# Hybrid decoder layer on one Trainium2 core: wider shift products and a tied order in the first stage, and five smaller moves behind it

## The chip, the core and the metric

The kernel runs on one core of a Trainium2 chip. The engines that matter are TensorE (PE; its weight loads are listed apart as PEld), VectorE (DVE), ScalarE (ACT), GpSimd (POOL, used here for fills and for issuing DMAs) and SyncE (SP, which issues most DMAs). They run side by side and wait for one another through semaphores. The metric is the device time of one execution in microseconds (us); lower is better. One profiled execution gives a trace with every instruction on every engine.

## The reference

One layer (DEPTH = 1) over 1024 tokens of width 1024: a mixing sub-layer that runs a convolution module and stick-breaking attention on one modulated input, then a SwiGLU sub-layer; all is float32.

```python
c_act = jax.nn.silu(c)
mod = c_act @ ada_w[l] + ada_b[l]
sh1, sc1, ga1, sh2, sc2, ga2 = [m[:, None, :] for m in jnp.split(mod, 6, axis=-1)]
h = rmsnorm(x, pre_mix_g[l]) * (1.0 + sc1) + sh1
y = hybrid_mixer(h, ...)
x = x + ga1 * rmsnorm(y, post_mix_g[l])
h = rmsnorm(x, pre_ffn_g[l]) * (1.0 + sc2) + sh2
y = swiglu_ffn(h, w_ffn_in[l], w_ffn_out[l])
x = x + ga2 * rmsnorm(y, post_ffn_g[l])
...
def hybrid_mixer(h, ...):
    proj = h @ w_in
    glu_in, qkv, gates = jnp.split(proj, [2 * CONV_WIDTH, 2 * CONV_WIDTH + 3 * ATT_WIDTH], axis=-1)
    ...
    merged = jax.nn.sigmoid(g_conv) * y_conv + jax.nn.sigmoid(g_att) * y_att
    return merged @ w_o
```

## The kernel before

Activations are kept transposed: 8 tiles of 128 channels by 1024 tokens, and a product works on one stationary block of 128 x 128 weights and 512 tokens (a chunk c, of two). For precision each float32 operand is split into a rounded part (hi, type float32r, made on ACT) and the remainder (lo, made on DVE), and a product is the sum of three: hi x hi, hi x lo and lo x hi. In the text these are named HH (weight hi, activation hi), HL (weight hi, activation lo) and LH (weight lo, activation hi). Plain float32 products (sums with a block of ones, shift products, convolution) go through PE in two records each.

The stages, in order of time:

- **First stage**, up to about 67 us. ACT squares the tiles of x, PE sums them over the channels with a block of ones (pvar). For each of the 8 channel tiles k a 1 MB tile of the conditioning weights (ada_w, `aws[k]`, five buffers) gives a shift and a scale. The scales of all k, and the shifts of k = 5 to 7 (SH_DVE), are dot products on DVE (`dots`, line 121). The shifts of k = 0 to 4 are made on PE: `shift_pe(k)` (L280) runs eight products of 128 x 128 weights with one moving column, and `shift_act(k)` (L284) adds the bias. `x_op` (DVE, L296) scales x, `hi_op` (ACT, L299) and `lo_op` (DVE, L302) make the split operand of h, and `gemm_k` (L317) multiplies it with three weight tiles: the first of Q, of K and of the gate of the convolution's GLU (q0b, k0b, gg0b; the weights are `w0s`). The loop over k does Q, K and gate of one k, each in the order HH, HL, LH. `pin` chains the instructions of an engine in the order of the program text, so that the planner can't reorder them; in this stage only DVE and ACT are pinned.
- **Attention and convolution**, to about 415 us. `qk_pair` copies Q and K out of PSUM (L499 to L516), `v_half` (L478) makes V with two weight tiles that `load_w` splits (L145, L155), `head` does the attention, `glu` and `conv` the convolution module.
- **Gates**, from about 410 us on. Two of the sixteen gate tiles are made plainly (PLAIN, L622) and stored to DRAM (`s_d`, L101); the other seven pairs go through a scheme with seven instead of eight block products (`early`, L635, and `other_five`, L704 to L731), in which the planner mixes the layer norm of the convolution (`ln_all`).
- **Projections**: `y_conv` (L747) with four weight tiles `wc`, the attention's projection, then w_o (L919). A weight tile goes through three rotations of three buffers each: raw ("wraw"), hi ("whi") and lo ("wlo"). The gate operands of `other_five` use the same "whi" and "wlo" buffers.
- **FFN**, from about 740 us. Its beginning is written out by hand and pinned on PE, DVE and ACT. While the second half of the tokens is still being normalised, PE makes early products for 11 of the 22 blocks: `ke(f, i)` (L1109) multiplies one weight tile with four operand tiles, and `e(f, i)` (L1114) copies the result out and stores it. The sums T1 to T4 of the seven-product scheme are made by `t12`, `t3` (L1134), `t4` with `hi_of` (ACT, L1119) and `lo_of` (DVE, L1123). `ffn(f)` is a generator: each `next(r0)` does one more step of block 0 (operands s2o, then s1o and s3o, then the products, L1001).
- **Last stage**, from about 1170 us: the second FFN product in four sweeps; the first, "pa", uses `prep1`, which splits two weight parts (`wop2`, L1535) and two activation parts (`op2`, L1529; L145 for both hi parts).

Outside the pinned pieces a planner orders every engine's instructions from a simulated timeline, with priorities that follow the program text. Each engine then runs its instructions strictly in that order. DMAs are issued by SP (loads, `load`), POOL (stores, `store`, L101) or ACT (`act.dma_start`).

## Time and profile before

| | |
|---|---|
| median of 3 runs | 1400.02 us (1399.16 to 1400.69) |
| the profiled execution | 1400.8 us |
| span in the profile (first to last instruction) | 1399.0 us |
| mean granted clock of PE over the span | 0.994 |
| instructions | 18714 |
| read from and written to HBM | 192.74 MB and 71.04 MB |

The times of the profile are counted from the span's start. A line of a timeline gives start, duration, engine, source line, operation, written and read tiles, shapes and count; in brackets stands the idle time of the engine before it and what ended it. PE's matmuls overlap, so the start of one to the start of the next is its cost, not its duration.

### The profile page before, as it was taken

What the parts mean: (1) busy time and instruction counts of PE and PEld (TensorE: products, weight loads), DVE (VectorE), ACT (ScalarE), POOL (GpSimd) and SP (SyncE); (2) the same over time, 40 slices, a digit from 0 to 9 for tenths busy, and PEclk for the clock granted to TensorE, in tenths of its full rate; (3) what the DMA queues carried; (4) which work ended last, traced back from release to release, by engine and by line L of the source; (5) the groups of instructions that cost most, each with busy time, mean ns of one, the idle gap of its engine ahead of it and who ended that gap; (6) DMA issues with size and microseconds to landing.
All of it is one profiled execution on the core that took longest, in us unless ns stands there. A gap on an engine that the chain in (4) does not pass through costs nothing.

```text
span 1399.0 us, 18714 instructions
## 1 busy us (share of the span) xinstructions
PE 1370.6 (98%) x6778; PEld 1150.3 (82%) x6778; DVE 1043.6 (75%) x1592; ACT 651.5 (47%) x1147; POOL 109.4 (8%) x251
## 2 busy tenths in 40 slices
PE   8999999999999999999999999999999999999996
PEld 5898898998987887888887778888888887888886
DVE  7898586775858789677597887778887876785355
ACT  6375465464546456213366553334454444433441
POOL 0100000000000011000012100001111110000002
PEclk8999999999999999999999999999999999999999
DMA  9512050141359646855845635457777779586736
GB/s 384 204 31 76 31 166 31 61 121 46 123 191 318 203 128 233 308 183 176 311 136 188 196 115 192 142 179 249 252 241 263 248 240 398 176 330 229 249 110 121
DMA packets 94684, 265.01 MB, mean 189 GB/s; under 512 B 10048, under 2 KB 21440, under 8 KB 93568
## 3 DMA queue, kind: packets, MB, share of 16 engines
q1 hardware_dynamic: 74352, 201.68, 43.2%
q0 software_dynamic: 18224, 58.47, 11.9%
q10 hardware_dynamic: 2016, 3.67, 0.7%
q8 instruction: 53, 0.87, 0.3%
q14 instruction: 39, 0.32, 0.1%
HBM read 192.74 MB, written 71.04 MB: 189 GB/s over the span
## 4 chain that ended last, share of the span: by engine, by line
PE 76%; issue 14%; DVE 3%; DMA 3%; ACT 2%; POOL 1%; POOLq 0%; DVEq 0%; SPq 0%; ACTq 0%
PE ka L1001 14%; PE ka L1543 9%; PE kc L1001 8%; PE pwo L919 5%; PE pb L1543 4%; PE pgv L166 3%; PE pyc L747 3%; PE pya L166 3%; PE pv L478 3%; PE pq L166 2%; PE pk L166 2%; PE pgg L166 2%; PE pa L1543 2%; PE kb L1001 2%; PE tr L574 2%
## 5 line engine op out<-in xcount | busy, mean ns | idle before, releaser
L550 ACT ACTIVATE ka<-z 128x128 f32<-128x128 f32 (+2 forms) x96 | 47.4, 496 | 53.0 <-PE z L549 43.7
L556 DVE TENSOR_TENSOR_SCAN ka<-ka,eye 128x128 f32<-128x128 f32 (+1 forms) x64 | 51.9, 824 | 17.1 <-ACT ka L550 17.1
L1543 PE MATMUL ka<-gt,w2f 128*128 128x512 f32 x264 | 63.4, 389 | 0.0
L121 DVE SCALAR_TENSOR_TENSOR ada<-ada,cb 128x1024 f32<-128x1024 f32 x32 | 39.0, 1223 | 27.5 <-DMA ada<-in_ada_dram 27.5
L1543 PEld LDWEIGHTS ka<-gt,w2f 128*128 128x128 f32 x264 | 49.6, 188 | 10.3
L561 DVE TENSOR_TENSOR be<-be,ka 128x127 f32<-128x127 f32 (+2 forms) x96 | 52.0, 553 | 7.2 <-ACT be L552 1.8
L1109 PE MATMUL ke<-b,w_hi 128*128 128x512 f32 x176 | 55.2, 395 | 0.0
L552 ACT ACTIVATE be<-z 128x127 f32<-128x127 f32 (+2 forms) x96 | 47.0, 496 | 3.9 <-PE tr L574 3.8
L574 PE MATMUL tr<-ident,be 128*128 128x128 f32 x288 | 47.3, 272 | 0.0
L559 DVE TENSOR_TENSOR_SCAN ka<-ka 128x512 f32<-128x512 f32 x32 | 40.4, 1274 | 4.3 <-ACT ka L550 4.2
L458 PE MATMUL pcv<-ph,cvw 128*128 128x128 f32 x320 | 43.1, 274 | 0.0
L458 PEld LDWEIGHTS pcv<-ph,cvw 128*128 128x128 f32 x320 | 40.6, 191 | 0.7
L1109 PEld LDWEIGHTS ke<-b,w_hi 128*128 128x128 f32 x176 | 32.9, 188 | 7.9 <-issue 0.7
L580 ACT ACTIVATE ahi<-tr 128x512 fp32r<-128x512 f32 x48 | 28.3, 600 | 23.1 <-PE tr L574 17.4
L145 ACT ACTIVATE gt<-X 128x512 fp32r<-128x512 f32 x33 | 20.3, 629 | 39.6 <-DVE X L1586 17.5
L581 DVE TENSOR_TENSOR alo<-tr,ahi 128x512 fp32r<-128x512 f32 x48 | 32.3, 684 | 8.5 <-ACT ahi L580 8.3
L478 PE MATMUL pv<-wv_hi,hhi 128*128 128x256 f32 x128 | 36.7, 287 | 1.6 <-DVE vst L483 0.9
L145 ACT ACTIVATE s1o<-s 128x512 fp32r<-128x512 f32 x22 | 13.8, 629 | 50.4 <-PE ka L1001 44.0
L574 PEld LDWEIGHTS tr<-ident,be 128*128 128x128 f32 x288 | 34.8, 140 | 2.8
L402 PE MATMUL k<-hhi,a 128*128 128x512 f32 x112 | 35.4, 391 | 1.7 <-ACT ee L635 1.6
L478 PE MATMUL pv<-wv_hi,hlo 128*128 128x256 f32 x128 | 36.7, 287 | 0.0
L478 PE MATMUL pv<-wv_lo,hhi 128*128 128x256 f32 x128 | 36.3, 285 | 0.0
(550 smaller groups left out, 4178.6 us busy)
## 6 DMA issues: line engine op xcount, KB each, us to landing
w_d<-w2o POOLq DMA_DIRECT2D x44, 512.0 KB, 7.5
w2f<-w_d SPq DMA_DIRECT2D x44, 512.0 KB, 4.3
ada<-in_ada_dram SPq DMA_DIRECT2D x32, 512.0 KB, 5.1
w2r<-in_w_dram SPq DMA_DIRECT2D x44, 256.0 KB, 3.8
w1g<-in_w_dram SPq DMA_DIRECT2D x21, 512.0 KB, 3.7
w1u<-in_w_dram SPq DMA_DIRECT2D x21, 512.0 KB, 5.7
cvw<-in_cvw_dram SPq DMA_DIRECT2D x20, 512.0 KB, 3.7
ada_w<-in_ada_dram SPq DMA_DIRECT2D x8, 1024.0 KB, 14.0
```

The source lines that it names most:

```text
L166: pe.matmul(bank, st[:, cols], mv[k][:, c * CH:(c + 1) * CH], start=(i == 0 and s == 0), stop=(i == n - 1 and s == 2))
L458: pe.matmul(cv[:, gi * TM:(gi + 1) * TM], wts[n][:, at:at + P], ph[:, g, SH - 1 - d:SH - 1 - d + TM], start=(d == 0), stop=(d == SH - 1))
L478: pe.matmul(pv[:, :256], st[k][:, tcols], mv[:, wc], start=(k == 0 and i == 0), stop=(k == KT - 1 and i == 2))
L550: act.activation(kap[:, s_lo:s_hi], z[:, zo:zo + w], AF.Sigmoid, bias=0.0, scale=-0.125)
L552: act.activation(beta[:, :m], z[:, zo:zo + m], AF.Sigmoid, bias=0.0, scale=0.125)
L556: dve.tensor_tensor_scan(rev, rev, eye[:, CH - w:][:, ::-1], 0.0, op0=ALU.mult, op1=ALU.add)
L561: dve.tensor_tensor(beta[:, :m], beta[:, :m], kap[:, s_lo + 1:s_lo + 1 + m], op=ALU.mult)
L574: pe.transpose(tr[:, o:o + P], probs[ii][:, jo:jo + P], ident)
L919: pe.matmul(bank_, st[:, cols], mv[k][:, cs], start=(k == 0 and q == 0), stop=(k == KT - 1 and q == 2))
L1001: pe.matmul(bank_, st[:, cols], t[:, mv], start=(first and j == 0 and s == 0), stop=(j == HK - 1 and s == 2), skip_group_check=not first)
L1109: pe.matmul(kbs[f], wes[f][st][:, cols], t[:, mv], start=(i == 0 and j == 0 and q == 0), stop=(j == HK - 1 and q == 2), skip_group_check=i ...
L1543: pe.matmul(dst, w[st][:, cols], g[mv], start=first and s == 0, stop=last and s == 2, skip_group_check=more)
```

## The change

**First stage.** `csb` is a new tile of eight blocks of 128 columns, each block one column of silu(c) repeated; DVE makes it after the sum for k = 2. The shift products use it as the moving operand, so each has 128 equal output columns, of which the first is read; `psh` has four such slots, used in turn. PE is pinned too, from `shift_pe(0)` on. `shift_pe` runs one tile further ahead. `gemm_k` is replaced by `gemm_q`, which does chosen ones of HH, HL and LH: the two HH products of Q for k = 0 come as soon as their half of h is there, with `shift_pe(2)` between them; later the HL products of one k come behind the HH and LH products of the next.

**V's first weights.** The two `load_w` calls for V move from `v_half(0)` into `qk_pair(0)`, each behind the copies of one half of Q, and this piece is pinned on DVE and ACT.

**Gate stores.** The plain gate tiles are stored by ACT's queue, not POOL's.

**Projection weight.** The first weight tile of `y_conv` is loaded and split ahead of the last gate pair, and its hi and lo parts have tiles of their own.

**FFN's early products.** `ke` does HH and HL of all four operand tiles first, then LH of all four.

**T3.** Its sums come ahead of block 0's first step, its lo parts ahead of `ke(9, 1)`.

**Last stage.** `prep1` makes both activation operands ahead of both weight operands.

```diff
-    def pin(start, engines=PINNED):
+    def pin(start, engines=PINNED, end=None):
         last = {}
-        for i in nc.cur_bb.bb.instructions[start:]:
+        for i in nc.cur_bb.bb.instructions[start:end]:
...
-        psh = ps0.tile([P, KT], F32, name="psh")
+        psh = ps0.tile([P, 4, P], F32, name="psh")
+        csb = p0.tile([P, KT, P], F32, name="csb")
...
                 dve.tensor_tensor(rstd, rstd, sq, op=ALU.add)
+                if k == 2:
+                    for kt in range(KT):
+                        dve.tensor_scalar(csb[:, kt], ones, csil[:, kt:kt + 1], None, op0=ALU.mult)
...
-                pe.matmul(psh[:, k:k + 1], aws[k][:, 0, kt * P:(kt + 1) * P], csil[:, kt:kt + 1],
+                pe.matmul(psh[:, k % 4], aws[k][:, 0, kt * P:(kt + 1) * P], csb[:, kt],
...
-        def gemm_k(b_, w, k):
+        def gemm_q(b_, w, k, *sms, cs=(0, 1)):
             cols = slice(k * P, (k + 1) * P)
-            for q, (st, mv) in enumerate(((0, 0), (0, 1), (1, 0))):
-                for c, bank_ in b_.items():
-                    pe.matmul(bank_, w[st][:, cols], h[mv][k][:, hs[c]], start=(k == 0 and q == 0),
-                              stop=(k == KT - 1 and q == 2))
+            for st, mv in sms:
+                for c in cs:
+                    pe.matmul(b_[c], w[st][:, cols], h[mv][k][:, hs[c]], start=(k == 0 and st == 0 and mv == 0),
+                              stop=(k == KT - 1 and mv == 1))
+
+        HH, HL, LH = (0, 0), (0, 1), (1, 0)
...
             x_op(0, hs[c])
             hi_op(0, hs[c])
+            gemm_q(q0b, w0s[0], 0, HH, cs=(c,))
+            if c == 0:
+                shift_pe(2)
...
-                if kn + 1 < KT and kn + 1 not in SH_DVE:
-                    shift_pe(kn + 1)
+                if kn + 2 < KT and kn + 2 not in SH_DVE:
+                    shift_pe(kn + 2)
...
-            ws = (q0b, k0b, gg0b)
-            if k <= 1:
-                for i in range(k + 1):
-                    gemm_k(ws[i], w0s[i], k)
-                for kk in range(k + 1):
-                    gemm_k(ws[k + 1], w0s[k + 1], kk)
+            ws = list(zip((q0b, k0b, gg0b), w0s))
+            if k == 0:
+                gemm_q(*ws[0], 0, LH, HL)
+                gemm_q(*ws[1], 0, HH, HL)
+            elif k == 1:
+                gemm_q(*ws[0], 1, HH, LH)
+                gemm_q(*ws[1], 0, LH)
+                gemm_q(*ws[1], 1, HH, LH)
+                gemm_q(*ws[2], 0, HH, HL)
+                gemm_q(*ws[2], 1, HH)
             else:
-                for b_, w_ in zip(ws, w0s):
-                    gemm_k(b_, w_, k)
+                for i, bw in enumerate(ws):
+                    if k == 2 and i == 2:
+                        gemm_q(*bw, 0, LH)
+                        gemm_q(*bw, 1, LH)
+                    gemm_q(*bw, k, HH, LH)
+                    if k == KT - 1:
+                        gemm_q(*bw, k - 1, HL)
+                        gemm_q(*bw, k, HL)
+                if k < KT - 1:
+                    for bw in ws:
+                        gemm_q(*bw, k - 1, HL)
         high.__exit__(None, None, None)
         pin(begin, START_PIN)
+        pin(pe_begin, PINNED[:1])
...
-                qk = qk_pair(0)
-            v = v_half(0)
+                begin = len(nc.cur_bb.bb.instructions)
+                wv0 = []
+                qk = qk_pair(0, lambda c: wv0.append(load_w(wv[0, c], f"wv0_{c}", act, dve)))
+                pin(begin, START_PIN)
+            v = v_half(0, wv0)
...
-                    store(s_d[n][:, c * CH:(c + 1) * CH], sg)
+                    act.dma_start(s_d[n][:, c * CH:(c + 1) * CH], sg)
...
         def y_conv(n):
-            if n % 2 == 0:
+            if n % 2 == 0 and n:
                 wcs[n // 2] = load_w(wcv[n // 2], f"wc{n}", act, dve)
...
             other_five(i)
+            if q == len(GPAIRS) - 2:
+                raw = wp.tile([P, T], F32, tag="wraw", name="wc0_raw")
+                load(raw, wcv[0])
+                wcs[0] = [pg.tile([P, T], F32R, name=f"wc0_{nm}") for nm in ("hi", "lo")]
+                copy_to(act, wcs[0][0], raw)
+                dve.tensor_tensor(wcs[0][1], raw, wcs[0][0], op=ALU.subtract)
...
-            for j in range(HK):
-                cols = slice(i * CH + j * P, i * CH + (j + 1) * P)
-                t = B[("B11", "B21")[i], j]
-                for q, (st, mv) in enumerate(((0, 0), (0, 1), (1, 0))):
-                    pe.matmul(kbs[f], wes[f][st][:, cols], t[:, mv], start=(i == 0 and j == 0 and q == 0),
-                              stop=(j == HK - 1 and q == 2), skip_group_check=i > 0)
+            for st, mvs in ((0, (0, 1)), (1, (0,))):
+                for j in range(HK):
+                    cols = slice(i * CH + j * P, i * CH + (j + 1) * P)
+                    t = B[("B11", "B21")[i], j]
+                    for mv in mvs:
+                        pe.matmul(kbs[f], wes[f][st][:, cols], t[:, mv],
+                                  start=(i == 0 and j == 0 and st == 0 and mv == 0),
+                                  stop=(j == HK - 1 and st == 1), skip_group_check=i > 0)
...
         ke(8, 1)
+        for j in range(HK):
+            t3(j)
         next(r0)
         e(8, 1)
-        for j in range(HK):
-            t3(j)
         ke(10, 0)
         e(10, 0)
+        for j in range(HK):
+            lo_of("T3", j, h2[j, 1])
         ke(9, 1)
         e(9, 1)
         next(r0)
-        for j in range(HK):
-            lo_of("T3", j, h2[j, 1])
         ke(10, 1)
...
-            return [(wop2(f"wa11_{j}", w[:, 0], act, dve), op2(f"gb11_{j}", x[:, 0], act, dve)),
-                    (wop2(f"wa12_{j}", w[:, 1], act, dve), op2(f"gb21_{j}", x[:, 1], act, dve))]
+            gs = [op2(f"gb{q}1_{j}", x[:, q - 1], act, dve) for q in (1, 2)]
+            return [(wop2(f"wa1{q}_{j}", w[:, q - 1], act, dve), gs[q - 1]) for q in (1, 2)]
```

More of the change, by code (lines that the diff above doesn't have):

```diff
@@ L279, in shift_pe @@
             for kt in range(KT):
[L280 removed]
+                pe.matmul(psh[:, k % 4], aws[k][:, 0, kt * P:(kt + 1) * P], csb[:, kt],
                           start=(kt == 0), stop=(kt == KT - 1))
         def shift_act(k):
[L284 removed]
+            act.activation(shift_of(k), psh[:, k % 4, 0:1], AF.Identity, bias=vec[:, C_ADAB + k:C_ADAB + k + 1], scale=1.0)
         def dots(k):
@@ L464, in conv, with v_half @@
                     load(u_d[ct][hf * (NG // 2):(hf + 1) * (NG // 2)].rearrange("g p m -> p g m"), o)
-            def v_half(hf):
-                w = [load_w(wv[hf, g], f"wv{hf}_{g}", act, pool if hf else dve) for g in range(2)]
+            def v_half(hf, w=None):
+                if w is None:
+                    w = [load_w(wv[hf, g], f"wv{hf}_{g}", act, pool if hf else dve) for g in range(2)]
                 tiles = []
@@ L485, in v_half, with qk_pair @@
                 return tiles
-            def qk_pair(p):
+            def qk_pair(p, between=None):
                 qs = [pc.tile([P, T], F32R, tag="qst", name=f"qst{p}_{i}", bufs=3) for i in range(2)]
@@ L502, in qk_pair @@
                     dve.tensor_tensor(qs[1][A, cs], b[c][B], qs[1][B, cs], op=ALU.subtract)
+                    if between:
+                        between(c)
                 if p == 0:
```

2 lines of the change are left out of this document (1 added, 1 removed).

## The prediction

> **What bounds the kernel now.** I read the busy shares first, then the waits of TensorE (PE) summed by cause, then the windows with the granted clock, then the timelines around each wait.
>
> ```profile
> PE 1370.6 (98%) x6778; PEld 1150.3 (82%) x6778; DVE 1043.6 (75%) x1592; ACT 651.5 (47%) x1147; POOL 109.4 (8%) x251
> PE pyc L747 <- ACT wc_hi L145: 2.1, 1, 2.1
> PE pq L317 <- ACT hhi L299: 2.0, 1, 2.0
> PE k L402 <- ACT ee L635: 1.6, 1, 1.6
> PE ke L1109 <- DVE w_lo L1043: 1.3, 2, 0.8
> ```
>
> The span is 1399.0 us and PE is busy in 1370.6 of it, so PE bounds nearly every stage and 28.4 us is idle. The page's definition warns that a busy PE need not be a PE at its peak, so there are two kinds of saving: the idle places (each row gives the total, the count and the longest; the four listed hold 7.0 us), and stretches in which PE is busy but slow. For the second kind the windows are read (busy of PE, PEld, DVE, ACT, POOL, then granted clock, DMA share, GB/s):
>
> ```profile
> 20.00:22.00 2.00, 1.64 (x16) 1.56 (x15) 1.86 (x4) 1.61 (x3) 0.00 (x0) 1.00 1.07 436
> 22.00:24.00 2.00, 0.98 (x7) 0.67 (x7) 1.93 (x3) 0.20 (x1) 0.00 (x0) 0.92 0.96 393
> 24.00:26.00 2.00, 1.05 (x4) 0.96 (x5) 1.96 (x5) 1.82 (x3) 0.72 (x1) 0.50 1.04 426
> 32.00:34.00 2.00, 2.00 (x9) 1.71 (x7) 1.97 (x4) 1.11 (x1) 0.53 (x1) 0.52 0.98 410
> ```
>
> The clock falls to half inside 22 to 24 us (a mean of 0.92 puts it at 23.7) and returns just before 34 (0.52 puts it at 33.9): 10.2 us at half speed, while PE is busy from 24.95 on. What PE did before the fall, and the end of the stage:
>
> ```profile
> 20.71 1.93 PE L280 MATMUL psh<-csil,ada_w 128*128 128x1 f32 x16 [0.36 <-ACT mod L284]
> 24.95 0.79 PE L317 MATMUL pq<-hhi,w0hi 128*128 128x512 f32 x1 [1.97 <-ACT hhi L299]
> 25.54 3.41 PE L280 MATMUL psh<-csil,ada_w 128*128 128x1 f32 x16
> 63.10 0.61 PE L317 MATMUL pq<-hhi,w0hi 128*128 128x512 f32 x2
> 66.73 0.61 PE L317 MATMUL pgg<-hhi,w0lo 128*128 128x512 f32 x2
> 68.11 0.36 PE L478 MATMUL pv<-wv_hi,hhi 128*128 128x256 f32 x1 [0.77 <-DVE qst L502]
> ```
>
> Eight shift products (16 records: float32 goes in two) with one moving column take 1.93 us at full clock and 3.41 at half; in columns streamed they are almost nothing. From 63.10 to 66.73 lie 16 of the 512-column products, so one is 0.227 us; the last pair started at 66.73 is through at 67.2.
>
> **The change, part by part.**
>
> *First stage.* The shift products get 128 equal columns. The nearest row for that is the convolution's product of the same shape:
>
> ```profile
> 187.91 2.17 PE L458 MATMUL pcv<-ph,cvw 128*128 128x128 f32 x18
> 3.22 1.66 DVE L240 TENSOR_SCALAR dia<-ident,csil 128x128 f32<-128x128 f32 x8
> 11.64 1.23 DVE L262 TENSOR_TENSOR rstd<-rstd,sq 128x1024 f32<-128x1024 f32 x1 [1.39 <-ACT sq L247]
> 56.81 2.59 DVE L302 SCALAR_TENSOR_TENSOR hlo<-x,mod,hhi 128x1024 fp32r<-128x1024 f32 x2
> 56.93 1.16 ACT L299 ACTIVATE hhi<-x,mod 128x1024 fp32r<-128x1024 f32 x1 [3.98 <-DVE x L296]
> ```
>
> 18 records in 2.17 us, less one record's 0.28 us of latency, is 0.111 us each: 16 make 1.8 us, as with one column (the weight loads, PEld, set the pace: busy 1.56 against PE's 1.64 in the window at 20). So the wider products cost PE nothing and fill it with streamed columns. The eight copies that build their moving operand (csb) cost 1.66 us of VectorE (DVE), by the eight of L240; they stand after the sum of k = 2, at about 10.3, ahead of an addition that has 1.39 us of idle before it, so 0.3 is left over. I take 0; without that idle place it would be 1.66.
>
> Does the clock stay up? In the 3 us before the fall at 23.7 PE streamed hardly more than one 512-column product (0.23 us): the rest were one-column records and idle time. After the change the same 3 us hold 1.8 of streaming from 20.7 on, plus that product: 2.0 of 3, two thirds. The idle time alone (1.97 us) isn't longer than what the new order leaves (waits to 24.4 and 28.15, below), so I take the missing columns for the cause, and the clock to stay up. The other reading is rival A.
>
> The order of PE is now pinned as written, so the DMAs of the shift weights can block it. Issues and landings (KB, us to landing) for k = 2 and, first of the four issues at 13.05, k = 3:
>
> ```profile
> 10.49 0.33 SPq L98 DMA_DIRECT2D ada_w<-in_ada_dram  x1
> ada_w<-in_ada_dram SPq DMA_DIRECT2D x1, 1024.0 KB, 13.9
> 13.05 12.64 SPq L98 DMA_DIRECT2D ada_w<-in_ada_dram  x4
> ada_w<-in_ada_dram SPq DMA_DIRECT2D x1, 1024.0 KB, 15.1
> ```
>
> They land at 24.4 and 28.15; another 3.8 us on, k = 4 lands at about 32 (an estimate from that spacing). shift_pe(2) now stands between the two first products and waits to 24.4; shift_pe(3) stands ahead of the k = 0 products and waits to 28.15, with those queued behind it. From there hardly anything is late (shift_pe(4) is reached 1.8 + 8 x 0.227 = 3.6 us later, at 31.8): 2 shift sets at 1.8 and 142 of the 144 products at 0.227 are 35.8 us, so PE ends at 64.0 against 67.2. The other bound is DVE, busy 1.93 to 1.97 of 2 us in those windows and in an order that doesn't change but for csb (the last hi operand is there at 58.1, the last lo at 59.4): from 58.1 there remain the k = 7 products and the low ones of k = 6, 24 of them, 5.4 us, so 63.5 at best. PE is the later one: **3.2 less**; I take 3.0, with 0.1 (below) and 3.65 as ends. If the landings were later, PE would pay them one for one.
>
> The V weights: the first copies now come after the first half of Q's copies, and since Q's last products now come 3.6 us ahead of the stage's end (16 of 0.227) rather than 2.7, four copies and two splits fit in. The 0.77 us before 68.11 should go: **0.8 less**, ends 0 and 0.9. Their splits on DVE and ACT are as many as before, and pinned only over this piece.
>
> *Gate stores.* Four stores go from POOL's queue to ACT's, each then about 0.33 us of ACT:
>
> ```profile
> s_d<-sg POOLq DMA_DIRECT2D x2, 256.0 KB, 5.0
> s_d<-ee ACTq DMA_DIRECT2D x2, 256.0 KB, 3.3
> 430.03 0.34 ACTq L636 DMA_DIRECT2D e_d<-ee  x1
> 437.18 0.58 ACT L635 ACTIVATE ee<-k 128x512 f32<-128x512 f32 x1
> ```
>
> The same 256 KB lands 1.7 us sooner from ACT's queue, and each store frees a buffer that an early copy waits for. But the last of them was issued between 425 and 427, so landed by 432, and PE's 1.6 us wait ends with the copy at 437.18: the store was long done. I take 0; ends 1.4 lost (four issues of 0.34) and 1.6 gained. [...]
>
> *Projection weight.* The copy that ends PE's longest wait:
>
> ```profile
> 520.00:540.00 20.00, 19.16 (x85) 15.53 (x84) 19.89 (x30) 15.06 (x21) 1.93 (x4) 1.00 0.45 131
> 552.88 1.52 PE L402 MATMUL kc<-T1o,s1o 128*128 128x512 f32 x6
> 556.46 0.50 PE L747 MATMUL pyc<-hhi,wc_hi 128*128 128x512 f32 x1 [2.06 <-ACT wc_hi L145]
> 555.36 1.04 ACT L145 ACTIVATE wc_hi<-wc_raw 128x1024 fp32r<-128x1024 f32 x1
> ```
>
> The raw tile keeps its place in its rotation (after the last gate pair, before the second projection weight), so its DMA starts as before. The copy took the buffer of a gate operand whose product is in the group at 552.88 or just ahead of it; in tiles of its own, it and its split (1.04 on ACT, and on DVE 1.23 like the addition of the same size at 11.64) run once the raw tile is there, and PE has ready products for the gap. The price: DVE is busy 19.89 of 20 us there, so 1.2 us of other splits shift; PE has the new products to cover them. **1.8 less**, ends 0 and 2.06.
>
> *Early products and T3.* PE waits 0.80 and 0.53 for the lo half of a weight:
>
> ```profile
> 786.46 0.50 PE L1109 MATMUL ke<-b,w_lo 128*128 128x512 f32 x1 [0.80 <-DVE w_lo L1043]
> 821.08 0.93 PE L1001 MATMUL ka<-T_0o,a 128*128 128x512 f32 x3 [0.47 <-DVE uw L1416]
> 801.48 0.69 DVE L992 TENSOR_TENSOR s2o<-s,s2o 128x512 fp32r<-128x512 f32 x1 [2.50 <-ACT s2o L145]
> 807.40 0.69 DVE L992 TENSOR_TENSOR s1o<-s,s1o 128x512 fp32r<-128x512 f32 x1 [2.58 <-ACT s1o L145]
> ```
>
> In ke the lo weight is now first read after 8 products (1.8 us) rather than 2 (0.45), which covers both waits: 1.3. T3's four sums (0.69 each by the DVE rows here, 2.8 us) go into the 2.50 idle before 801.48 and its four lo parts (2.8) into the 2.58 before 807.40; DVE is then ahead, and the 0.47 wait shrinks. **1.7 less**; ends 0 (if DVE's row of work up to 821.08 doesn't move, the wait there takes up what the earlier ones give) and 1.8 (1.33 + 0.47). No DMA moves past another; e(8,1) and its store stand behind four more ACT copies, and the bank it frees isn't needed at once.
>
> *Last stage.* The two activation operands now precede the weights:
>
> ```profile
> 1020.00:1040.00 20.00, 20.00 (x90) 16.58 (x89) 15.77 (x27) 9.53 (x17) 3.24 (x6) 1.00 0.71 240
> 1169.98 0.63 ACT L145 ACTIVATE wa<-wa 128x512 fp32r<-128x512 f32 x1 [1.36 <-PE ka L1001]
> 1170.51 2.70 ACT L145 ACTIVATE gb<-X 128x512 fp32r<-128x512 f32 x5
> 1171.18 1.19 PE L1543 MATMUL ka<-gb,wa 128*128 128x512 f32 x4 [1.24 <-ACT gb L145]
> ```
>
> The sixth weight copy waits for PE's last FFN product and five activation copies stand behind it. Put first, they run in ACT's idle time. **1.0 less**, ends 0.4 (PE may then wait for a PSUM bank that DVE, not ACT, frees last) and 1.24.
>
> **Sum:** 3.0 + 0.8 + 0 + 1.8 + 1.7 + 1.0 = 8.3. The profiled execution took 1400.8 us (1399.0 and 1.8 around it), 0.8 over the median of 1400.02. So 1392.5 for it, **1391.7** as a median. The window at 1020, like most behind the places named, shows PE busy 20.00 of 20 us, so what is won is kept.
>
> **Rivals.** (A) *The clock falls all the same*, because the waits to 24.4 and 28.15 leave PE too little in a stretch. Then from 28.2 to 33.9 it does half of 5.7 us: 2.9 lost, first-stage gain 0.1, time 1394.6. Against it: two thirds of the 3 us stream. [...] (C) *DVE takes over at 520 to 560 and 800 to 820*: the waits there only change their name, and the 1.8 + 1.7 are not won: 1395.2. For it: 19.89 of 20 busy. (B) *The planner's order*: outside the pinned pieces an automatic plan orders every engine from its own timeline, and an earlier first stage can give another order through attention and gates, 77 to 560 us, where DVE and ACT copies release PE's banks. Such a wait costs 0.8 to 1.6 (the rows of qst and ee); five of 0.8 eat half the gain, more than ten eat it all, and with 14 the time is 1402.9, slower. Against it: nothing of the attention is edited, and fourteen such waits would hold more than the four causes listed first.
>
> **How the numbers follow.** Forecast 0.56, A with A' 0.12, C 0.12, B 0.20 (0.13 of it a near tie, 0.07 slower). A measurement can tell about 0.2%, 2.8 us, from no change. Faster: 0.56 + 0.12 + 0.12 = 0.80, same 0.13, slower 0.07. The range goes from all upper ends (3.65 + 0.9 + 1.6 + 2.06 + 1.8 + 1.24 = 11.3, so 1388.7) to 1397.2, where B begins.
>
> **What would show it.** Right: clock 1.00 in every window from 20 to 36; first V product at about 64 to 65; no PE wait named wc_hi, w_lo or gb. Wrong: 0.50 anywhere there (A), the same waits under other names (C), new bank waits between 77 and 560 (B).

## The result, and the profile after

The changed kernel takes 1392.91 us (median of 6 runs, 1392.09 to 1394.07) against 1400.20 of the kernel before (6 runs beside it). The ratio is 0.9943, 95% interval 0.9930 to 0.9955, which is 6.3 to 9.8 us less (7.3 by the medians), and the two profiled executions agree: 1391.1 us of span against 1399.0, 7.9 less. The forecast was 1391.7, with 8.3 less. One run of the experiments (the old product order) took 1522 us at a mean clock of 0.85, and it is left out below.

The busy times on the page of the changed kernel:

```profile
PE 1364.4 (98%) x6778; PEld 1146.5 (82%) x6778; DVE 1046.8 (75%) x1600; ACT 651.6 (47%) x1147; POOL 107.1 (8%) x247
```

There are as many PE instructions as before. PE is busy 6.2 us less and idle 1.7 less (26.7 against 28.4). Of the 6.2, about 4.5 are the half-speed time of the first stage (PE was busy in 9 us of the 10.2 at half clock). So the larger part of the gain is PE time that was slow, not PE time that was empty; waits that went are in part made up by new ones. PE's waits by cause (total, times, longest):

```profile
PE psh L284 <- DMA ada_w<-in_ada_dram: 2.8, 2, 1.6
PE k L426 <- ACT ee L665: 1.6, 1, 1.6
PE ka L1581 <- ACT gb L145: 1.2, 1, 1.2
PE ke L1146 <- ACT w_hi L145: 1.1, 1, 1.1
```

Here ee is the copy of an early gate product out of PSUM, gb an activation operand of the last stage and w_hi the rounded part of an FFN weight. The waits named wc_hi, w_lo and qst are gone. New are the two for the shift weights' DMAs and one for w_hi. The wait for gb, which the change aimed at, is as it was. The windows of the first stage, where the third number from the end is the granted clock (1.00), show no fall:

```profile
22.00:24.00 2.00, 1.41 (x12) 1.10 (x10) 1.83 (x4) 0.63 (x2) 0.00 (x0) 1.00 1.00 410
...
26.00:28.00 2.00, 0.97 (x8) 0.66 (x6) 2.00 (x2) 1.21 (x2) 0.00 (x0) 1.00 1.01 422
```

PE is idle for 1.03 us of the window from 26 to 28, yet the clock stays at 1.00, there and in all windows up to PE's last product. Places that can be set beside the kernel before are in PE's timeline, first of the changed kernel, then of the kernel before:

```profile
18.82 1.95 PE L284 MATMUL psh<-csb,ada_w 128*128 128x128 f32 x16
...
59.90 1.07 PE L321 MATMUL pq<-hlo,w0hi 128*128 128x512 f32 x4
...
64.43 0.28 PE L503 MATMUL pv<-wv_hi,hhi 128*128 128x256 f32 x1
...
433.97 0.50 PE L426 MATMUL k<-hhi,a 128*128 128x512 f32 x1 [1.61 <-ACT ee L665]
...
787.37 2.11 PE L1146 MATMUL ke<-b,w_hi 128*128 128x512 f32 x8 [1.07 <-ACT w_hi L145]
...
812.85 0.94 PE L1037 MATMUL ka<-T_0o,a 128*128 128x512 f32 x3 [0.46 <-DVE uw L1454]
...
1162.96 1.20 PE L1581 MATMUL ka<-gb,wa 128*128 128x512 f32 x4 [1.24 <-ACT gb L145]
```

```profile
437.81 0.50 PE L402 MATMUL k<-hhi,a 128*128 128x512 f32 x1 [1.61 <-ACT ee L635]
...
608.27 0.61 PE L166 MATMUL pya<-ohi,wa_hi 128*128 128x512 f32 x2
```

How much earlier each place comes in the changed kernel (s2o is the product before which PE waits for s2o, an operand of the seven-product scheme; pya and ke are the first products of the attention's projection and of the early FFN products; uw is a sum that VectorE makes of finished FFN products):

| place | before | after | gained so far | gained since the place above |
|---|---|---|---|---|
| first V product | 68.11 | 64.43 | 3.68 | 3.68 |
| k, with its wait of 1.61 | 437.81 | 433.97 | 3.84 | 0.16 |
| s2o | 527.81 | 523.87 | 3.94 | 0.10 |
| pya | 608.27 | 601.99 | 6.28 | 2.34 |
| ke | 741.10 | 734.64 | 6.46 | 0.18 |
| ka, wait for uw | 821.08 | 812.85 | 8.23 | 1.77 |
| last stage, wait for gb | 1171.18 | 1162.96 | 8.22 | -0.01 |

The gain comes in three steps, 3.7 in the first stage, 2.3 at the projection and 1.8 in the FFN's beginning. From 813 on nothing is won, and 0.3 are lost after the last stage's beginning.

### The profile page after: what moved, and what is told of

Same layout as the page of the kernel before. It is cut to its first block, busy times and chain, and to the rows that moved or that the text cites. A ratio compares the mean times of both kernels' runs of the same rounds, so it can differ in the third digit from the quotient of the medians.

```text
span 1391.1 us, 18714 instructions
## 1 busy us (share of the span) xinstructions
PE 1364.4 (98%) x6778; PEld 1146.5 (82%) x6778; DVE 1046.8 (75%) x1600; ACT 651.6 (47%) x1147; POOL 107.1 (8%) x247
## 4 chain that ended last, share of the span: by engine, by line
PE 93%; DMA 2%; ACT 2%; DVE 2%; issue 1%; SPq 0%; DVEq 0%; ACTq 0%
PE ka L1037 15%; PE ka L1581 9%; PE kc L1037 8%; PE pwo L955 6%; PE pb L1581 4%; PE ke L1146 4%; PE ka L426 4%; PE pgv L166 3%; PE pya L166 3%; PE pyc L777 3%; PE pv L503 3%; PE kc L426 2%; PE k L426 2%; PE pgg L166 2%; PE pk L166 2%; PE pcv L482 2%
## 5 line engine op out<-in xcount | busy, mean ns | idle before, releaser
L1146 PE MATMUL ke<-b,w_hi 128*128 128x512 f32 x176 | 44.5, 395 | 1.1 <-ACT w_hi L145 1.1
```

The source lines that it names most:

```text
L1146: pe.matmul(kbs[f], wes[f][st][:, cols], t[:, mv], start=(i == 0 and j == 0 and st == 0 and mv == 0), stop=(j == HK - 1 and st == 1), skip ...
```

## The experiments

Ratios are to runs of the kernel before on the same chip. Where the position of a place is compared, it is counted from the start of the first shift set on PE, since that start lies between 18.2 and 19.1 us in the executions, also of kernels that are the same up to there (the waits for the squares sq ahead of it differ, from 0.3 to 2.2 us in all).

### One column in the changed order

```diff
-                pe.matmul(psh[:, k % 4], aws[k][:, 0, kt * P:(kt + 1) * P], csb[:, kt],
+                pe.matmul(psh[:, k % 4, 0:1], aws[k][:, 0, kt * P:(kt + 1) * P], csil[:, kt:kt + 1],
```

> The changed kernel with the shift products' moving operand one column wide again (order of PE, copies for csb and everything else as changed). Theory 'streamed columns hold the clock': 0.1 us of streaming per shift set brings the clock down to 0.50 for some 10 us between 22 and 36, although PE's order is the changed one; the first V product starts at about 67 instead of 64.43, and the time is about 3 us longer (1395.9 against 1392.9). Rival 'the order alone did it' (idle places and not columns set the clock, or the time was lost in waits for operands): clock 1.00 in all windows from 20 to 38, first V product at 64.4, time unchanged. Between them (first V product at 65 to 66): the clock falls, but shorter or later.

Ratio to before 0.9982 (0.9968 to 0.9997), median 1400.03 us. Windows and PE's timeline of this kernel:

```profile
24.00:26.00 2.00, 1.00 (x5) 1.00 (x5) 1.97 (x4) 0.72 (x1) 0.72 (x1) 0.55 1.04 426
...
44.00:46.00 2.00, 2.00 (x9) 1.63 (x8) 1.96 (x5) 0.00 (x0) 0.00 (x0) 0.83 1.04 426
```

```profile
19.12 1.84 PE L284 MATMUL psh<-csil,ada_w 128*128 128x1 f32 x16
...
72.22 0.28 PE L503 MATMUL pv<-wv_hi,hhi 128*128 128x256 f32 x1
...
442.06 0.50 PE L426 MATMUL k<-hhi,a 128*128 128x512 f32 x1 [1.61 <-ACT ee L665]
```

Every window between these two shows 0.50. With the mean of 0.55 and of 0.83 that makes 1.8 + 18 + 0.68 = 20.5 us at half clock, twice as long as before. The first V product comes 53.1 us after the first shift set, against 45.6 in the changed kernel. So the order alone does not hold the clock. One column cost more than I expected, since the fall can be longer: the ten runs lie in two groups, three of 1395.8 to 1397.0 with a mean clock of 0.992, and seven of 1399.9 to 1401.6 with 0.990 or less. The three would fit the 3 us that I expected.

### 128 columns in the order of before

Beside the line below, `psh` has its four slots, and csb is made as in the changed kernel.

```diff
-                pe.matmul(psh[:, k:k + 1], aws[k][:, 0, kt * P:(kt + 1) * P], csil[:, kt:kt + 1],
+                pe.matmul(psh[:, k % 4], aws[k][:, 0, kt * P:(kt + 1) * P], csb[:, kt],
```

> The kernel before with nothing but 128 equal columns in the shift products (and the eight copies that make them); PE's order is the planner's as before. Theory 'columns hold the clock, and the pinned order adds little to it': clock 1.00 from 20 to 38, first V product at 64.5 to 65.5 instead of 68.11 less the 0.8 of the V weights' wait that this kernel still has (so the wait before it about 0.8), time 2.5 to 3.2 us under before. Rival 'the order is needed too': the clock still falls, or it stays up and PE still ends at 67 or later because it waits for operands; the first V product is within 1 us of 68.1 and the time that of before within 1 us.

Ratio 0.9996 (0.9985 to 1.0006): the time can't be told from that of before. Windows, then PE's timeline:

```profile
24.00:26.00 2.00, 1.23 (x7) 1.22 (x8) 1.96 (x4) 1.82 (x3) 0.72 (x1) 0.85 1.04 426
26.00:28.00 2.00, 2.00 (x11) 2.00 (x11) 2.00 (x3) 0.00 (x0) 0.00 (x0) 0.50 1.03 422
28.00:30.00 2.00, 2.00 (x10) 1.70 (x9) 2.00 (x3) 1.02 (x1) 0.57 (x1) 0.80 1.00 410
```

```profile
24.77 0.50 PE L321 MATMUL pq<-hhi,w0hi 128*128 128x512 f32 x1 [1.85 <-ACT hhi L303]
...
50.46 0.73 PE L321 MATMUL pq<-hlo,w0hi 128*128 128x512 f32 x2 [0.76 <-DVE hlo L306]
...
64.12 0.61 PE L321 MATMUL pq<-hhi,w0lo 128*128 128x512 f32 x2
...
68.23 0.36 PE L482 MATMUL pv<-wv_hi,hhi 128*128 128x256 f32 x1 [1.45 <-DVE qst L506]
...
436.56 0.50 PE L406 MATMUL k<-hhi,a 128*128 128x512 f32 x1 [1.61 <-ACT ee L639]
```

The half-clock time shrinks from 10.2 to 3.4 us (0.3 + 2 x 0.5 + 0.4 of full-clock time lost in the three windows, over 0.5), so PE has about 2.8 us more (in the first 1.2 us of the fall before it stood idle, where half speed cost nothing). It spends most of that in waits: for hlo, which VectorE delivers at its own pace and the order HH, HL, LH needs at once (twice, 1.5 us in all), and then 1.45 instead of 0.77 for qst, because Q's last pair starts at 64.12, as in the kernel before (64.01). The first V product waits for Q's copies and splits, not for PE's last product. In the changed order Q's last group starts at 59.90. The first V product is not all, though: the place of the wait for ee comes 418.2 us after the first shift set (18.34) here and 419.3 in the kernel before, so 1.1 us of gain come to light behind the first V product.

By that place, the wide columns alone are worth 1.1 us, the order with one column (and the V weights early) costs 3.6 (442.06 - 19.12 = 422.9), and both together are worth 4.2, of which 1.3 are the V weights' (below). The wide columns give PE time; the order, with the HL products one k later and Q ahead of K and gate at the end, lets it use that time. Columns alone do not keep the clock up, either: behind the idle place of 1.85 us ahead of 24.77 it still fell for 3.4 us.

### 32 columns

```diff
-                pe.matmul(psh[:, k % 4], aws[k][:, 0, kt * P:(kt + 1) * P], csb[:, kt],
+                pe.matmul(psh[:, k % 4, 0:32], aws[k][:, 0, kt * P:(kt + 1) * P], csb[:, kt, 0:32],
```

> The changed kernel with 32 instead of 128 equal columns in the shift products: as many matmuls and weight loads, a quarter of the streaming. If the clock follows the share of streamed columns in its window, the shift sets stream 0.45 us instead of 1.8 and the clock falls in the window from 22 to 28 (0.50 in at least one stretch of 3.4 us), first V product 2 to 6 us later than 45.6 us behind the first shift set. If it takes little more than the one column of before to hold it, clock 1.00 throughout and first V product 45.6 us behind the first shift set, as in the changed kernel.

Ratio 0.9980 (0.9969 to 0.9992), median 1396.64. A window, and the timeline:

```profile
20.00:22.00 2.00, 1.65 (x11) 1.54 (x11) 1.86 (x4) 1.80 (x3) 0.00 (x0) 0.75 1.05 430
```

```profile
18.29 1.87 PE L284 MATMUL psh<-csb,ada_w 128*128 128x32 f32 x16
20.51 3.21 PE L284 MATMUL psh<-csb,ada_w 128*128 128x32 f32 x16 [0.35 <-ACT mod L288]
```

A quarter of the columns does not hold it. PE had no idle place over 0.35 us since 12.7, and the clock falls in the second shift set (0.75 from 20 to 22, then 0.50 in every window to 34), sooner than I expected. From the changed kernel only the number of columns differs, and all nine runs have a mean clock of 0.994 or less against 0.997 there. So here the clock goes by what streams, not by whether PE has instructions. Where between 32 and 128 columns the bound lies was not tried. The first V product comes 48.8 us after the first shift set (67.08), 3.2 late, and the median is 3.7 over that of the kernel with T3's moves undone, which ran on the same chip (1392.91, below).

### The changed kernel again, and the V weights at their old place

```diff
-                qk = qk_pair(0, lambda c: wv0.append(load_w(wv[0, c], f"wv0_{c}", act, dve)))
-                pin(begin, START_PIN)
-            v = v_half(0, wv0)
+                qk = qk_pair(0)
+            v = v_half(0)
```

> The changed kernel itself, beside the others on one chip. If its gain belongs to the kernel and not to the chip: ratio to before 0.9943 as at first (0.993 to 0.9955), no fall of the granted clock between 18 us and the end, and a spread of its own runs smaller than that of before, since before has the clock's fall, whose length differs between executions, and this kernel has none.

> The changed kernel with the first two V weights copied and split where the kernel before has them (behind all of the first pair's Q and K copies, not pinned). Theory: ACT and DVE then have the V weights later, PE waits before the first V product, which comes 0.8 us (0 to 0.9) later than in the changed kernel, at about 65.2; time 0.8 longer. Rival 'the end of the Q products sets the first V product, and with Q ending at 60.8 instead of 64.5 the weights are early enough anyhow': first V product within 0.2 us of the changed kernel's, time the same.

The changed kernel gives 0.9943 again (0.9928 to 0.9957), its six runs 1392.41 to 1395.06 with a mean clock of 0.997 each; the 11 runs of before 1399.43 to 1405.55 with 0.994 down to 0.989. Its gain is that of the kernel, and its runs lie closer together (2.7 us against 6.1). What varies in it, too, is shown by this run's timelines of PE and VectorE:

```profile
525.12 2.60 PE L426 MATMUL ka<-T2o,s2o 128*128 128x512 f32 x10 [1.59 <-DVE s2o L413]
```

```profile
516.23 0.69 DVE L743 TENSOR_TENSOR gs<-gw5b 128x512 f32<-128x512 f32 x1 [3.64 <-DMA gw5b<-in_win_dram]
```

In the first profile of the changed kernel the wait for s2o was 0.38, and VectorE's step at L743 began at 514.78. Its weight gw5b landed 1.45 us later this time (issued 0.4 later, and 5.0 us on the way instead of 4.0), VectorE has no long idle time from there to s2o, and PE pays 1.2 of it.

Without the V edit the ratio is 0.9952 (0.9935 to 0.9969), the median 1394.84, 1.3 over the changed kernel beside it. PE's timeline:

```profile
63.83 0.30 PE L503 MATMUL pv<-wv_hi,hhi 128*128 128x256 f32 x1
...
65.55 0.38 PE L503 MATMUL pv<-wv_lo,hhi 128*128 128x256 f32 x1 [0.69 <-DVE wv_lo L155]
...
69.08 0.36 PE L503 MATMUL pv<-wv_hi,hhi 128*128 128x256 f32 x1 [0.88 <-DVE klo L543]
...
73.22 0.44 PE L575 MATMUL z<-kst,qst 128*128 128x384 f32 x1 [0.77 <-ACT be L579]
```

The rival was right about the first V product: it starts 45.6 us after the first shift set (18.24) with and without the edit. But then PE waits three times: for the lo weight, whose split now stands behind all four Q splits on VectorE; for klo, K's remainder (0.88 instead of 0.22); and for be, an operand of the first attention head. At the wait for ee (434.73 here) this kernel is 370.9 us behind its first V product, the changed one 369.5. The edit is worth 1.4, behind the place at which I looked for it.

### The fourth and fifth shift set later

```diff
-                if kn + 2 < KT and kn + 2 not in SH_DVE:
-                    shift_pe(kn + 2)
...
                 gemm_q(*ws[1], 0, HH, HL)
+                shift_pe(3)
             elif k == 1:
+                shift_pe(4)
```

> The changed kernel with the fourth and fifth shift sets later in PE's order (the fourth behind the low products of k = 0, the fifth right after it), so that PE does not stand before the DMA of the fourth weight with products behind it. Theory 'the first stage now ends with VectorE's last operands': the wait of 1.58 us for that DMA shrinks to under 0.5, but first Q end and first V product move by less than 0.5 us. Rival 'PE's order around the DMAs is the bound': first V product 1.0 to 1.6 us sooner (about 63). Third case: the idle place of 1.58 plus later work lets the clock fall.

Ratio 0.9942 (0.9927 to 0.9957), as the changed kernel. PE's timeline:

```profile
27.65 0.73 PE L321 MATMUL pq<-hlo,w0hi 128*128 128x512 f32 x2 [0.47 <-DVE hlo L306]
...
31.44 2.05 PE L284 MATMUL psh<-csb,ada_w 128*128 128x128 f32 x16 [0.35 <-ACT mod L288]
33.25 0.70 PE L321 MATMUL pq<-hhi,w0hi 128*128 128x512 f32 x2
...
63.73 0.28 PE L503 MATMUL pv<-wv_hi,hhi 128*128 128x256 f32 x1
```

The wait of 1.58 for the DMA is gone, and the first V product comes 45.5 us after the first shift set (18.25) instead of 45.6. The number is the one that the theory gave, but its reason is not what the rows show. From 33.25 to the first V product PE has no wait, and VectorE's last lo operand is done at 59.15, about 0.5 before PE reads it: the end of this stage is PE's. What was won at the DMA went to other places ahead of 33.25: PE now waits for VectorE's first lo operand (hlo, 0.47) and for ACT between two shift sets in a row (0.35), with smaller gaps beside them. From the second HH product to the first product of k = 1 it takes 7.34 us (25.91 to 33.25), in the changed kernel 7.47 (26.49 to 33.96). So removing this DMA wait is worth 0.1 in this order. An order in which the two shift sets stand apart was not run.

### The projection weight in the old rotation

```diff
-            if q == len(GPAIRS) - 2:
-                raw = wp.tile([P, T], F32, tag="wraw", name="wc0_raw")
...
-            if n % 2 == 0 and n:
+            if n % 2 == 0:
                 wcs[n // 2] = load_w(wcv[n // 2], f"wc{n}", act, dve)
```

> The changed kernel with the projection's first weight loaded and split at its old place again (rotating buffers). Theory: PE's wait of about 2.1 us for wc_hi ahead of the first projection product returns, and the stretch up to the projection's end is 2.1 to 2.4 us longer than in the changed kernel; time about 1395.2. Rival 'DVE holds this stage': PE's waits in 523 to 610 add up to the same in both, and the time moves by less than 0.5.

Ratio 0.9969 (0.9959 to 0.9979), median 1396.65. PE's timeline and windows:

```profile
525.84 2.57 PE L426 MATMUL ka<-T2o,s2o 128*128 128x512 f32 x10 [2.15 <-DVE s2o L413]
...
554.52 0.50 PE L777 MATMUL pyc<-hhi,wc_hi 128*128 128x512 f32 x1 [2.09 <-ACT wc_hi L145]
...
607.96 0.62 PE L166 MATMUL pya<-ohi,wa_hi 128*128 128x512 f32 x2
```

```profile
554.00:556.00 2.00, 1.48 (x6) 1.26 (x7) 2.00 (x4) 0.99 (x2) 0.54 (x1) 0.97 1.03 424
556.00:558.00 2.00, 2.00 (x6) 1.51 (x6) 0.66 (x2) 0.00 (x0) 0.00 (x0) 0.50 1.02 418
558.00:560.00 2.00, 2.00 (x8) 1.59 (x7) 0.00 (x0) 0.00 (x0) 0.00 (x0) 0.68 1.02 416
```

The wait is back, and in this execution the clock falls behind it for 3.4 us (0.06 + 1.0 + 0.64 lost, over 0.5), which costs 1.7 more. From s2o to pya (behind the wait of 2.15, which is another one that varies) it takes 82.1 us, in the changed kernel 78.1: 4.0, of which 1.7 are the clock and 2.3 the wait. Not every execution need have the fall. The kernel before and the one with 128 columns in the old order have waits of 2.06 and 2.12 us at the same product, and their profiles show 1.00 in the windows behind it. Four of the ten runs here lie at 1395.4 to 1395.8, 2.5 to 2.9 over the changed kernel's 1392.91 (from another chip), the others at 1396.5 to 1399.6; which of these had the fall is not seen.

### FFN: the product order, T3, and the new wait

The old order of the early products:

```diff
-            for st, mvs in ((0, (0, 1)), (1, (0,))):
-                for j in range(HK):
...
+            for j in range(HK):
+                cols = slice(i * CH + j * P, i * CH + (j + 1) * P)
+                t = B[("B11", "B21")[i], j]
+                for q, (st, mv) in enumerate(((0, 0), (0, 1), (1, 0))):
...
```

> The changed kernel with the early FFN products in the order of before again (for each row block: hi by hi, hi by lo, lo by hi), T3's moves kept. Theory: the lo weights are needed 6 products earlier, so PE's two waits for w_lo (0.80 and 0.53 in the kernel before) return and the one of 1.07 us for w_hi goes, because it only stands in their place; from the stretch's start (ke at about 734.6) to the product at 812.85 it takes 0.2 to 1.6 us longer than the changed kernel. Rival: 'the new order gains nothing, the 1.07 us for w_hi gives it all back': the stretch is as long as in the changed kernel within 0.2 us, and T3's moves made the whole gain of 1.7.

Its one profile is of the run of 1522 us, so only three times are used: 1393.75, 1393.83 and 1394.60, ratio 0.9950 (0.9934 to 0.9967). The median of the three is 0.9 and 1.3 over those of two other kernels on the same chip (T3's moves undone, gate stores back). So the product order is worth about 1, by three runs, and the wait for w_hi does not give it all back. The stretch itself is not seen at full clock, so which wait returned stays open.

T3's moves undone:

```diff
-        for j in range(HK):
-            t3(j)
         next(r0)
         e(8, 1)
+        for j in range(HK):
+            t3(j)
...
-        for j in range(HK):
-            lo_of("T3", j, h2[j, 1])
         ke(9, 1)
         e(9, 1)
         next(r0)
+        for j in range(HK):
+            lo_of("T3", j, h2[j, 1])
```

> The changed kernel with T3's sums and lo parts where the kernel before has them, the new product order kept. Theory of the prediction: the sums only fill idle time of VectorE, so without the move VectorE is late at the end of the stretch: the wait of 0.46 us for uw before the product at 812.85 grows by 0.5 to 1.3, the time with it. Rival: 'T3's moves do nothing here, since no product waits for T3 at either place': stretch and time unchanged within 0.2 us.

Ratio 0.9942 (0.9925 to 0.9959), median 1392.91. PE's timeline, where the wait for uw is as long as in the changed kernel:

```profile
523.37 2.56 PE L426 MATMUL ka<-T2o,s2o 128*128 128x512 f32 x10 [0.69 <-DVE s2o L413]
...
812.87 0.93 PE L1037 MATMUL ka<-T_0o,a 128*128 128x512 f32 x3 [0.45 <-DVE uw L1454]
```

The stretch between these two is 289.5 us, against 289.0 in the changed kernel and in seven other profiles with T3's moves (288.96 to 289.04). So the moves give 0.5, in gaps too small to be listed, and too little for the times to show. Neither theory had that: the wait for uw did not grow, and the stretch is not the same within 0.2. Of the 1.77 won in the FFN's beginning about 1.3 are left for the product order, near what its own times say.

Then the wait of 1.07 for w_hi, which is new. On ACT, w_hi (at 786.28) stood behind four copies for T4 and T1, of which the first waited for VectorE until 784.04. One step is moved:

```diff
-        for j in range(2):
-            t4(j)
-        for j in (0, 1):
-            hi_of("T1", j, h2[j, 0])
         ke(6, 1)
         wh(9)
+        for j in range(2):
+            t4(j)
+        for j in (0, 1):
+            hi_of("T1", j, h2[j, 0])
         e(6, 1)
```

> The changed kernel with one step moved: the copy of the tenth early FFN weight (w_hi, ACT) and the product that frees its buffer are issued ahead of T4's and T1's first parts, nothing else. Theory 'PE's wait of 1.07 us at 787 is ACT's order: w_hi stands behind four copies that wait for VectorE': the wait goes, the first product after it starts about 1.3 us sooner and all later stages too; time 1.0 to 1.3 us shorter. Rival C of the prediction 'VectorE holds this stretch': the wait at 787 goes, but the one at 812.85 (for uw, 0.46 us) grows by as much, and the span stays within 0.3 us.

Ratio 0.9930 (0.9915 to 0.9945); the five runs, 1391.49 to 1392.31, all lie under the six of the changed kernel beside it (1392.41 to 1395.06). ACT's timeline, then PE's:

```profile
781.92 1.06 ACT L145 ACTIVATE w_hi<-w_raw 128x1024 fp32r<-128x1024 f32 x1 [0.15 <-PE ke L1146]
```

```profile
523.04 2.57 PE L426 MATMUL ka<-T2o,s2o 128*128 128x512 f32 x10 [0.38 <-DVE s2o L413]
...
810.68 0.94 PE L1037 MATMUL ka<-T_0o,a 128*128 128x512 f32 x3 [0.48 <-DVE uw L1454]
```

w_hi is made in idle time, 3.5 us sooner when both are counted from s2o, the wait goes, and the stretch takes 287.6 us, 1.3 less. The wait for uw at 810 does not grow, so VectorE does not hold this stretch. In this execution 0.8 are lost again at 972 (0.53 of wait for uw and the restart), where VectorE had waited for a weight's DMA. This is the best version that was run, about 1.8 us under the changed kernel and 9 under the one before by the medians (1391.73 against 1393.55 and 1401.14).

### Gate stores back on POOL's queue

```diff
-                    act.dma_start(s_d[n][:, c * CH:(c + 1) * CH], sg)
+                    store(s_d[n][:, c * CH:(c + 1) * CH], sg)
```

> The changed kernel with the four plain gate stores on the queue of before (POOL's). Theory: no product waits for these stores, so PE's wait of 1.61 us for ee stays as it is and the time is the same within 0.3 us. Rival 1: stores that land 1.7 us later hold the buffers that the early copies need, PE's wait near 434 grows by up to 1.6. Rival 2: four issues fewer on ACT, 1.3 us sooner.

Ratio 0.9942 (0.9927 to 0.9957), median 1392.54. The wait is the same to the hundredth:

```profile
433.66 0.50 PE L426 MATMUL k<-hhi,a 128*128 128x512 f32 x1 [1.61 <-ACT ee L665]
```

A second wait, of 0.73, comes 6.5 us later, and it does not show in the time.

### The last stage pinned to its text

```diff
+                if name == "pa" and j == 0:
+                    begin = len(nc.cur_bb.bb.instructions)
                 ops = prep(j, ahead.popleft())
+                if name == "pa" and j == 2:
+                    pin(begin, START_PIN)
```

> The changed kernel with ACT and DVE pinned to the written order over the operands of the last stage's first three steps, so that the activation copies gb really stand ahead of the weight copies wa. Theory 'the order on ACT makes PE's wait of 1.24 us for gb': ACT issues gb before the wa copies that wait for buffers, the wait goes, time 1.0 to 1.5 us shorter. Rival 'the weight copy is the late one' (it waits for a buffer that PE frees last, and PE needs it for the same product): the wait changes its name to wa and stays 0.5 to 1.3; time unchanged within 0.5, or longer if DVE now waits in the pinned order.

In the changed kernel ACT does six copies wa, three of them after a wait for PE, and only then gb. The last of the six and the row of gb:

```profile
1161.76 0.63 ACT L145 ACTIVATE wa<-wa 128x512 fp32r<-128x512 f32 x1 [1.36 <-PE ka L1037]
1162.29 2.70 ACT L145 ACTIVATE gb<-X 128x512 fp32r<-128x512 f32 x5
```

The second row is, but for its start, the row of before: the new text order of `prep1` did not reach the engine. Outside the pinned pieces the planner sets the order. With the pin, gb comes first, at 1160.18. PE's timeline, then ACT's:

```profile
1161.89 0.50 PE L1581 MATMUL ka<-gb,wa 128*128 128x512 f32 x1 [0.29 <-ACT wa L145]
1162.98 1.87 PE L1581 MATMUL ka<-gb,wa 128*128 128x512 f32 x7 [0.59 <-DVE gb L1567]
...
1181.46 0.50 PE L1581 MATMUL ka<-gb,wa 128*128 128x512 f32 x1 [2.10 <-ACT gb L145]
```

```profile
1180.26 0.63 ACT L145 ACTIVATE wa<-wa 128x512 fp32r<-128x512 f32 x1 [10.98 <-DMA wa<-in_w_dram]
```

The first wait falls from 1.24 to 0.29 and 0.59. But the planner also moved the loads of wa on SP: the fourth is issued at 1170.71, in the changed kernel at 1152.84. So ACT, pinned, stands 10.98 us before the next wa, and PE waits 2.10 at 1181. The ratio is 0.9974 (0.9963 to 0.9986), slower than the changed kernel; eight of the ten runs have a mean clock of 0.996 rather than 0.997 and 1397.1 to 1399.5 us, which would fit a half-clock stretch behind that wait (an estimate: 0.001 of 1394 us is 1.4 us, near the 1.7 that the stretch of 3.4 us cost above), though the profiled execution (1395.57, clock 0.997) has none: from 1182.26 eleven products take 2.60 us, 0.236 each. Neither theory was right: the order does make the wait, but pinning it alone gives more back.

## Why the prediction was right, and where not

**The first stage, 3.0, and the V weights, 0.8.** The sum was right (3.8 forecast, 3.84 at the place of the wait for ee), and so were the clock at 1.00 and the first V product "at about 64 to 65". The split was off: counted from the first shift set to that wait, the V edit is worth 1.3 to 1.4 and the rest of the stage about 2.8 (419.30 us before, 416.49 without the V edit, 415.15 with both). The step that mis-sized it was "the 0.77 us before 68.11 should go": the row of 0.77 names qst, Q's split, and that wait goes with the order alone, as the run without the V edit shows; the weights were not late for the first product but for those behind it. The reason for the clock, the missing columns, held with one and with 32 columns in the new order. It was not the whole reason: with 128 columns in the old order the clock still fell for 3.4 us. What the text did not see is that columns and order need each other; it priced the order only by what it makes late. Nor is the wait for the second of the two DMAs a price of its own: without its 1.58 us the stage was 0.1 shorter.

**Rival A** fell: the clock stayed up in the first stage of every profile used here that has 128 columns and the new order, with idle places of 1.27 and 1.58 us. **Rival A'**, that the fall isn't in every execution, was thought unlikely since the three runs lay within 1.5 us; three were too few to show how much the fall varies. In the 31 runs of before on another chip the times reach from 1398.51 to 1405.85, and the mean clock goes with them, 0.994 at the lower end and 0.989 at the upper. The profile with its fall of 10.2 us has 0.994, the changed kernel 0.997 or more. So by the mean clocks a fall is in every execution, but its length isn't fixed (where the longer ones lie no profile shows), and the measured gain depends on the runs of before that it is set against. The 3.0 was worked out from an execution with one of the shorter falls without knowing it; that is luck. The falls that the profiles show last 3.4 us at 128 columns in the old order and behind the wait in the run with the old weight rotation, 10.2 before and 20.5 with one column in the new order; what sets these lengths no run shows.

**Gate stores, 0.** Right, for the reason given.

**Projection weight, 1.8.** The mechanism was right, the size 2.34. A likely reading of the difference is that the idle time in the row isn't all that a wait costs. The 2.06 us stand between the modelled end of a 0.39 us product and the next start, while products follow each other at 0.227. So 0.16 of the last product lies outside the pitch, and the first product after the wait takes 0.33 to the next (556.46 to 556.79) instead of 0.227: 0.27 more than the row says, together 2.33. The 1.2 us of VectorE work that were to shift cost nothing there, so rival C has no case here.

**FFN, 1.7.** Right in size, 1.77 measured. Its parts weren't as told: the two w_lo waits went, T3's moves gave 0.5 without touching the wait for uw, and a wait of 1.07 for w_hi came in, which the text did not name. The step that missed it asked whether VectorE would be late and not what stood ahead of ACT's copy. Moving that copy gave 1.3, and the wait for VectorE's uw did not grow, which is against rival C here, too.

**Last stage, 1.0.** Wrong: nothing was won. The failed step is "Put first, they run in ACT's idle time": the text order was taken for the engine's order in a piece that isn't pinned. The row of ACT is the same in both kernels.

**Rival B** didn't happen: between 77 and 560 us the changed kernel's first profile has no wait over 0.45 that the kernel before hasn't (the wait for s2o, 0.84 before and 0.38 there, was 1.59 in its second). The sum was then too high by 1.0 in the last stage and 0.3 at the end, and too low by 0.5 at the projection, 0.1 in the FFN and 0.3 in the stretches between: 8.3 against 7.9 in the spans. That these cancel to within 0.4 is luck; the mechanisms that were right are those of the first stage, the projection and the w_lo waits.

## What to carry to other kernels

A TensorE that is busy with narrow matmuls can still lose its clock, as here (0.50 with one and with 32 columns): look at the granted clock before looking at idle time, and fill the columns where they cost little (here 0.1 us in a shift set, 1.95 against 1.84). When one engine is freed, check at once which order lets it use the time; two edits of which one alone is worth 1 us and the other alone costs 4 gave 4 together. Judge an edit at a place well behind it, too: the V weights and the wide columns showed their worth only behind the first V product. And in a program whose order is planned, look at the engine's rows for the order, not at the text.

## What was not expected of the hardware

- 32 columns in each shift product (16 records in 1.87 us, near the 1.95 with 128 columns) weren't enough to keep the clock (0.50 in every window from 22 to 34), 128 in the same order were (1.00).
- An idle place of 2.1 us between dense products had a half-clock stretch of 3.4 us behind it in one case (2.09 us) and none in four others (2.06 and 2.12 us, with 1.00 in the windows behind them, 2.10 and 2.15 us, with the next products 0.23 to 0.24 us apart); places of 1.27 and 1.58 us with shift sets of 128 columns around them had none in the profiles above.
- The landing of one 512 KB weight (gw5b) differed by 1.45 us between two executions of the same kernel, 1.0 of it on the way, and 1.2 of it reached PE.
